# Second block's experts: eight in fixed places, twenty-four ranked on the chip and loaded by register, six pairs and five quads in place of sixteen pairs

## The chip, the core and the metric

The kernel runs on one core of one Trainium2 chip. The metric is the time of one execution on the device in microseconds; the change is compared with the kernel before it on the same chip.

A core has several engines, each with an instruction queue of its own that it works through in order: TensorE (PE; its weight loads are shown apart as PEld), VectorE (DVE), ScalarE (ACT), GpSimd (POOL) and SyncE (SP). SP issues nearly all transfers here. They run on the core's 16 DMA engines.

## What is computed

Two transformer blocks stand one behind the other, for 256 tokens of 1024 channels. The first has one layer, with 16 experts that choose their tokens. The second has two layers, and each ends in the mixture of experts that the change is about: every token picks one of four groups and two of that group's eight experts, each of which is a gated product with 256 hidden columns.

```python
def hier_moe(x, rg_w, rg_b, re_w, re_b, w_gate, w_up, w_down):
    ...
    lg = jnp.einsum('td,dg->tg', t, rg_w, ...) + rg_b
    g_star = jnp.argmax(lg, -1)
    ...
    top_v, top_i = lax.top_k(le, TOP_K_IN_GROUP)          # 2 of the group's 8
    ...
    for g in range(N_GROUPS):
        h = silu(einsum('td,edf->tef', t, w_gate[g])) * einsum('td,edf->tef', t, w_up[g])
        y = y + jnp.einsum('tef,efd->td', h * gate[:, g, :, None], w_down[g])
```

All values are float32. So 512 pairs of token and expert fall on 32 experts, 16 on average, and how many an expert gets is known only when the router has run. Every expert's weights are 3 MiB: 1 MiB each of gate, up and down, 96 MiB per layer.

## The kernel before

Each layer of the second block is a mixer (`mixer2`), the router (`route2_logits`, `route2`, L2031) and a round of experts (`moe2_round`, L2115). The round does not compute all tokens with all experts. It gives every expert `CAP` = 48 places, followed by 16 of no use, so that an expert takes 64 columns. If an expert has more tokens than 48, a further round runs over all experts (the loop at L2342); `nrounds` says how many, and all engines read it into a register at L2340 and branch at L2341.

Within a round:

- `gather(oc)`, for eight experts at a time: VectorE writes the one-hot matrix S (L2127) by comparing slot numbers with `key`, TensorE multiplies the tokens' two float32r parts xh and xl with it (tile `ga`), ScalarE and VectorE evacuate the result in turn to `xsT` (L2136, L2139).
- `onehot(qd)`, for four experts: S transposed (`GT`, copied to `G`) and the gates of the slots (`gs`).
- `gate_up(pr)`, for a pair of experts: 16 products that accumulate in one bank `pg`, the first expert's slots on partitions 0 to 63, the second's on 64 to 127. ScalarE and VectorE make `hid` of it (L2177, L2178). TensorE takes gate_up of the next pair ahead of the rest of this one.
- `hid_transposed(pr)`: two transposes (`hT`), copied by VectorE to `hidT` (L2186).
- `down(pr)`: 8 products into two banks `py`, evacuated in two float32r parts `yhl` (L2201, L2202) that are scaled with the gates.
- `scatter(pr)`: 8 products `sct` of G and yhl, which VectorE adds to `y` (L2216).

A float32 product of 512 columns shows as two records of 128x512 in the trace.

The weights come in loads of 1 MiB ([128, 2048] floats): per expert two for gate and up (half the rows each, gate and up side by side) and one for down. `loads2` (L2102) lists them in the order of use: gate and up of pair 0, then of each further pair with down of the pair before. `plan` takes the list; `fetch` issues some ahead into slots; `next_w` hands out the next load that was issued, or, once those are used up, issues one into the slot whose turn it is (`fetch_one`, L253). There are 17 slots in turn (nine `ring`, seven `ringb` and the tile XT2), and two tiles that serve once (`wx`). By the time the round starts, 19 loads have been issued. All further ones stand on SP's queue, each with a wait for the products that read its slot last.

Around the first gather, the order of work on all engines but SP is the scheduler's from the point `order.__exit__` on; what stands ahead of it stands in the order of the code. `residual` (L2317) makes `y` ALPHA times the layer norm's result in two halves, whose vectors are loaded; the second half's are issued from GpSimd. `gates` (L2076) works out the gates and `nrounds`; it is called by the first `onehot`.

The first block's experts (`moe1`) work in groups of four, each with 32 slots: four products side by side on 32 columns each. Their weights are loaded in the same slots.

## Time and profile before

| | us |
|---|---|
| three runs | 1740.32, 1737.74, 1728.4 |
| median | 1737.74 |
| span of the profiled execution | 1736.4 |

| engine | busy us | share of the span |
|---|---|---|
| PE | 1587.0 | 91% |
| PEld | 828.7 | 48% |
| DVE | 746.9 | 43% |
| ACT | 391.6 | 23% |
| POOL | 228.1 | 13% |

No time of the profiled execution other than its span is given. HBM was read at 286 GB/s over the span, 495 MB in all.

How to read the profile: the timeline lists instructions of an engine in order of time, like ones merged, with what ended an idle time in square brackets. A line number is that of the kernel; L308 is the helper through which all products go, L312 the one for transposes, so tiles tell them apart. Windows give each engine's busy time in a stretch, TensorE's granted clock (1.00 is the upper of its two levels), and the share and rate of the DMA engines. Products on TensorE are pipelined, so a busy TensorE is not one at its peak, and products side by side overlap in the records.

### The profile page before, as it was taken

The numbers are of one execution on the slowest core, as the hardware profiler recorded it, in microseconds if no ns is written. First come the engines' busy times: TensorE is split into PE (matmuls) and PEld (weight loads), VectorE is DVE, ScalarE is ACT, GpSimd is POOL, SyncE is SP. The second block draws the span as 40 slices with busy tenths as digits, with TensorE's granted clock in tenths as the row PEclk, the third lists the DMA queues.
The fourth block names the chain that finished last, engine by engine and source line by source line (L and its number), as shares of the span: only waits on it lengthen the run. The fifth ranks groups of instructions, "written<-read, shape, count | busy, mean of one in ns | idle before, by whom it ended". The sixth has DMA issues, their size and how long they took to land. (4 is left out here: it accounts for less than half of the span.)

```text
span 1736.4 us, 19979 instructions
## 1 busy us (share of the span) xinstructions
PE 1587.0 (91%) x7819; PEld 828.7 (48%) x7825; DVE 746.9 (43%) x1552; ACT 391.6 (23%) x740; POOL 228.1 (13%) x147
## 2 busy tenths in 40 slices
PE   8969899988898888899998999999899999999996
PEld 3738775221241221267777454343567875444432
DVE  6798774010010000189446343232796545433325
ACT  2443333000000000055443111111445432111101
POOL 2362531000000000031212000000231211000000
PEclk8879999999989999999999999999989999999998
DMA  8446666999999999933456899984243737998860
GB/s 350 170 131 245 259 262 260 417 418 418 417 417 418 417 419 418 393 116 146 169 207 242 327 377 360 374 338 156 77 149 122 278 124 305 376 408 340 343 271 25
DMA packets 110229, 497.49 MB, mean 287 GB/s; under 512 B 9082, under 2 KB 9719, under 8 KB 88874
## 3 DMA queue, kind: packets, MB, share of 16 engines
q1 hardware_dynamic: 108904, 492.75, 72.0%
q10 hardware_dynamic: 690, 2.10, 0.3%
q0 software_dynamic: 528, 1.23, 0.3%
q8 instruction: 65, 1.06, 0.2%
q14 instruction: 42, 0.34, 0.1%
HBM read 495.00 MB, written 1.05 MB: 286 GB/s over the span
## 5 line engine op out<-in xcount | busy, mean ns | idle before, releaser
L308 PE MATMUL pg<-w,xsT 128*64 128x512 f32 (+1 forms) x1504 | 375.2, 602 | 17.4 <-DMA w<-in_w_gate_dram 15.6
L308 PEld LDWEIGHTS pg<-w,xsT 128*64 128x64 f32 (+1 forms) x1504 | 105.2, 128 | 232.2 <-issue 184.7
L266 POOL TENSOR_TENSOR wl<-w,wh 128x1024 fp32r<-128x1024 f32 x47 | 116.9, 2487 | 363.4 <-ACT wh L265 250.6
L308 PE MATMUL py<-w,hidT 128*64 128x512 f32 x496 | 152.8, 601 | 3.7 <-DVE hid L2178 3.7
L308 PE MATMUL py<-w,hh 128*32 128x512 f32 x512 | 128.7, 599 | 25.0 <-DMA w<-in_w_down_dram 25.0
L308 PE MATMUL pu<-w,xsT 128*32 128x512 f32 x512 | 126.2, 598 | 19.8 <-DMA w<-in_w_up_dram 19.8
L265 ACT ACTIVATE wh<-w 128x1024 fp32r<-128x1024 f32 x98 | 103.1, 1059 | 128.9 <-PE pj L308 56.2
L308 PE MATMUL pj<-wh,xTp 128*128 128x512 f32 (+1 forms) x448 | 123.7, 407 | 0.9 <-ACT cn L1718 0.9
L1397 DVE TENSOR_TENSOR hh<-hh,pu 128x512 f32<-128x512 f32 x8 | 5.4, 686 | 218.4 <-PE pu L308 218.4
L266 DVE TENSOR_TENSOR wl<-w,wh 128x1024 fp32r<-128x1024 f32 x51 | 73.4, 1439 | 58.7 <-ACT wh L265 38.5
L2202 DVE SCALAR_TENSOR_TENSOR yhl<-py,gs,yhl 128x512 fp32r<-128x512 f32 x64 | 47.8, 749 | 107.5 <-ACT yhl L2201 107.5
L308 PEld LDWEIGHTS pj<-wh,xTp 128*128 128x128 f32 x448 | 80.8, 198 | 19.4 <-issue 3.6
L308 PEld LDWEIGHTS py<-w,hh 128*32 128x32 f32 x512 | 29.3, 108 | 120.5 <-DMA w<-in_w_down_dram 66.1
L2216 DVE TENSOR_TENSOR y<-y,sct 128x512 f32<-128x512 f32 x128 | 81.9, 681 | 10.6 <-PE sct L308 10.5
L1396 ACT ACTIVATE hh<-pg 128x512 f32<-128x512 f32 x8 | 4.8, 597 | 344.8 <-PE pg L308 234.1
L308 PEld LDWEIGHTS py<-w,hidT 128*64 128x64 f32 x496 | 47.2, 136 | 71.9 <-issue 53.7
L308 PE MATMUL sct<-yhl,G 128*128 128x512 f32 x256 | 78.6, 428 | 0.0
L2177 ACT ACTIVATE hid<-pg 128x256 f32<-128x256 f32 x32 | 12.3, 385 | 286.8 <-PE pg L308 286.8
L2201 ACT ACTIVATE yhl<-py,gs 128x512 fp32r<-128x512 f32 x64 | 43.8, 688 | 144.9 <-PE py L308 128.0
L308 PEld LDWEIGHTS pu<-w,xsT 128*32 128x32 f32 x512 | 28.3, 109 | 100.3 <-DMA w<-in_w_up_dram 51.3
L1421 DVE SCALAR_TENSOR_TENSOR y<-py,gs,m 128x512 f32<-128x512 f32 x8 | 6.0, 750 | 148.9 <-PE py L308 148.5
L308 PEld LDWEIGHTS sct<-yhl,G 128*128 128x128 f32 x256 | 41.6, 188 | 50.9 <-DVE y L2216 19.5
(638 smaller groups left out, 2426.3 us busy)
## 6 DMA issues: line engine op xcount, KB each, us to landing
w<-in_expert_w_gate_up_dram SPq DMA_DIRECT2D x126, 1024.0 KB, 8.5
w<-in_w_up_dram SPq DMA_DIRECT2D x64, 1024.0 KB, 18.0
w<-in_w_down_dram SPq DMA_DIRECT2D x64, 1024.0 KB, 18.1
w<-in_w_gate_dram SPq DMA_DIRECT2D x62, 1024.0 KB, 18.4
w<-in_expert_w_down_dram SPq DMA_DIRECT2D x62, 1024.0 KB, 7.0
w<-in_w_in_dram SPq DMA_DIRECT2D x38, 1024.0 KB, 4.9
wmod<-in_w_ada_dram SPq DMA_DIRECT2D x12, 1024.0 KB, 5.4
wmod<-in_w_ada_dram SPq DMA_DIRECT2D x13, 512.0 KB, 9.3
```

What stands on the lines that cost most here:

```text
L265: nc.scalar.activation(hi, src, AF.Copy)
L266: (eng or nc.vector).tensor_tensor(lo, src, hi.bitcast(F32), ALU.subtract)
L308: self.nc.tensor.matmul(out, lhsT, rhs, start=start, stop=stop)
L1396: nc.scalar.activation(hs, pg[nb], AF.Silu)
L1397: nc.vector.tensor_mul(hs, hs, pu[nb])
L1421: nc.vector.scalar_tensor_tensor(y[:, cs], py[nb], Gs[g][1], m5[:, cs], op0=ALU.mult, op1=ALU.mult)
L2177: nc.scalar.activation(hid, pg[:, 0:256], AF.Silu)
L2201: nc.scalar.activation(yh[:, c], py, AF.Copy, scale=gs[:, pr % 2:pr % 2 + 1])
L2202: nc.vector.scalar_tensor_tensor(yl[:, c], py, gs[:, pr % 2:pr % 2 + 1], yh[:, c].bitcast(F32), op0=ALU.mult, op1=ALU.subtract)
L2216: nc.vector.tensor_add(acc[:, t, c], acc[:, t, c], pt)
```

## The change

The 32 experts get places in an order of their own. Places 0 to 7 are experts 0 to 7, as before. Places 8 to 31 are the other 24 in the order of how many tokens they have, fullest first. Places 0 to 11 (the eight fixed and the four fullest) have 64 slots each and work in six pairs; places 12 to 31 have 32 slots and work in five quads, four experts side by side on 32 columns. Eleven groups take the place of sixteen.

The ranks are worked out by VectorE in `order` (in `route2`): a score of each expert, its comparison with the 23 others, the sum as rank, the 24 x 24 permutation, and by products with it and sums (`pick`) the experts' numbers `ids` in order and the columns of `key` (`keyd`). `gates` also makes the gates' columns in order (`gated`) and compares the counts with the rooms of 64 or 32 for `nrounds`.

The loads of places 8 to 31 need `ids`. `loads2` gives a function for each load; at the first load of a group of four places SP reads four numbers into registers (`TENSOR_LOAD ids`), and each load's address is worked out from one (an `ISA` row ahead of each). The down weights are laid out in DRAM as one run of 8 KB per partition instead of two of 4 KB. Gathers serve three groups (384 columns, as before), four per round; the one-hots are made for a group at a time, and the first scatter stands behind the second down. A further round, should one be needed, goes over all experts in 16 pairs of 64 slots.

```diff
-CAP = 48
+NS, NB, BIG, SMALL = 8, 4, 64, 32
+GROUPS = [(BIG, (i, i + 1)) for i in range(0, NS + NB, 2)] + [(SMALL, tuple(range(i, i + 4))) for i in range(NS + NB, 32, 4)]
+FURTHER = [(BIG, (i, i + 1)) for i in range(0, 32, 2)]
...
     def fetch_one(self):
         src, shape = self.todo.popleft()
+        if callable(src):
+            src = src()
...
+        def pick(out, src):
+            for i in range(0, n, n // 2):
+                js = slice(i, i + n // 2)
+                tm = q.tile([128, n // 2, n], F32, name="picked")
+                nc.vector.tensor_tensor(tm, perm[:, js], src[:, None, :].to_broadcast([128, n // 2, n]), ALU.mult)
+                nc.vector.tensor_reduce(out[:, js], tm, axis=AX.X, op=ALU.add)
+
+        def order():
+            sc = q.tile([128, 32], F32, name="score")
+            nc.vector.scalar_tensor_tensor(sc, count, 32.0, self.iota[:, 0:32], op0=ALU.mult, op1=ALU.subtract)
+            for i in range(0, n, n // 2):
+                js = slice(i, i + n // 2)
+                tm = q.tile([128, n // 2, n], F32, name="picked")
+                nc.vector.tensor_tensor(tm, sc[:, None, NS:].to_broadcast([128, n // 2, n]),
+                                        sc[:, NS:][:, js, None].to_broadcast([128, n // 2, n]), ALU.is_gt)
+                nc.vector.tensor_reduce(rank[:, js], tm, axis=AX.X, op=ALU.add)
+            nc.vector.tensor_tensor(perm, self.iota[:, 0:n, None].to_broadcast([128, n, n]),
+                                    rank[:, None, :].to_broadcast([128, n, n]), ALU.is_equal)
...
+            pick(idf, self.iota[:, NS:32])
+            nc.vector.tensor_copy(ids, idf)
+            for t in range(2):
+                pick(keyd[:, t], key[:, t, NS:])
...
         def gates():
...
             nc.vector.tensor_add(gate, oh[:, :, 0], oh[:, :, 1])
+            for t in range(2):
+                pick(gated[:, t], gate[:, t, NS:])
...
-    def loads2(self, l):
+    def loads2(self, l, groups, ids=None):
+        def expert(i):
+            if i < NS or ids is None:
+                return i
+            if i not in named:
+                c = i - NS
+                _, vs = nc.values_load_multi_w_load_instructions(
+                    ids()[0:1, c:c + 4], [mybir.EngineType.SP], min_val=NS, max_val=31, ...
+                named.update({i + j: v for j, v in enumerate(vs)})
+            return named[i]
...
+            return gu_[l, bass.ds(e, 1), h].rearrange("o p (k c) -> p (o k) c", k=4)
...
-        return gu(0) + [a for pr in range(1, 16) for a in gu(pr) + d(pr - 1)] + d(15)
+        return gu(0) + [a for g in range(1, n) for a in gu(g) + d(g - 1)] + d(n - 1)
...
-                wt = [self.next_w() for _ in range(2)]
+                wt = [self.next_w() for _ in places]
                 for k in range(4 * h, 4 * h + 4):
-                    for j in range(2):
-                        self.mm(pg[64 * j:64 * j + 64, :], xsT[:, k, (e + j) * CAP:(e + j) * CAP + 64], wt[j][:, k % 4, :],
-                                start=(k == 0), stop=(k == 7))
+                    for j, w in enumerate(wt):
+                        c = slice(n * j, n * j + n)
+                        self.mm(pg[c, :], xsT[:, k, c], w[:, k % 4, :], start=(k == 0), stop=(k == 7))
...
         gate_up(0)
+        if residual:
+            r.order()
+            r.gates()
         onehot(0)
...
-        for pr in range(16):
-            if pr < 15:
-                gate_up(pr + 1)
-            hidT = hid_transposed(pr)
-            if pr:
-                scatter(pr - 1)
-            if pr % 4 == 2 and pr < 14:
-                gather(pr // 4 + 1)
-            if pr % 2 == 0 and pr < 14:
-                onehot(pr // 2 + 1)
-            down(pr, hidT)
-        scatter(15)
+        for g in range(last + 1):
+            if g < last:
+                gate_up(g + 1)
+            hidT = hid_transposed(g)
+            if g > 1:
+                scatter(g - 1)
+            if g < last:
+                onehot(g + 1)
+            if g % 3 == 1 and g + 2 <= last:
+                gather(g + 2)
+            down(g, hidT)
+            if g == 1:
+                scatter(0)
+        scatter(last)
```

How this moves instructions is shown at three places of the first layer's round, the kernel before first and the changed kernel second each time. The first is VectorE's queue at the round's start, from the residual's second half to the copy `hidT` of the first group, for which the first down product waits. Before:

```order
L2328 SCALAR_TENSOR_TENSOR y_3855<-y_3855,gb_5821 128x512 x2
L2329 SCALAR_TENSOR_TENSOR y_3855<-gb_5821,y_3855 128x512
L2155 CAST G_5871<-GT_5872 128x512
L2161 COPY gs_5870<-gs_5878 128x2
L2329 SCALAR_TENSOR_TENSOR y_3855<-gb_5821,y_3855 128x512
L2178 TENSOR_TENSOR hid_5842<-hid_5842,pg_5825 128x256
L2186 COPY hidT_5915<-hT_5912 128x256
```

And in the change, from the first `hid` on:

```order
L2271 TENSOR_TENSOR hid_5847<-hid_5847,pg_5830 128x256
L2095 TENSOR_TENSOR picked<-perm,routes 128x288
L2254 COPY gs_5920<-gs_5926 128x1
L2427 SCALAR_TENSOR_TENSOR y_3855<-gb_5826,y_3855 128x512
L2096 TENSOR_REDUCE byrank_5743<-picked 128x12
L2426 SCALAR_TENSOR_TENSOR y_3855<-y_3855,gb_5826 128x512
L2095 TENSOR_TENSOR picked<-perm,routes 128x288
L2427 SCALAR_TENSOR_TENSOR y_3855<-gb_5826,y_3855 128x512
L2096 TENSOR_REDUCE byrank_5743<-picked 128x12
```

Behind these nine rows stand two more pairs of `picked` and `byrank_5743`, the second group's `hid`, and only then `hidT` of the first; ahead of them, from the first gather's last evacuation on, stand the rest of the ranking and the residual.

The second place is TensorE's queue from the first group's transposes on. Before:

```order
L312 MATMUL hT_5912<-ident,hid_5842 128x128 x2
L312 MATMUL GT_5919<-ident,S_5763 128x128 x4
L308 MATMUL gs_5925<-routes,S_5763 64x1 x8
L308 MATMUL py_5936<-w,hidT_5915 64x512 x4
L308 MATMUL py_5943<-w,hidT_5915 64x512 x4
L308 MATMUL pg_5950<-w,xsT_5764 64x512 x16
L312 MATMUL hT_5970<-ident,hid_5909 128x128 x2
L308 MATMUL pg_6006<-w,xsT_5764 64x512
```

In the change:

```order
L318 MATMUL hT_5956<-ident,hid_5847 128x128 x2
L318 MATMUL GT_5963<-ident,S_5769 128x128 x2
L314 MATMUL gs_5967<-routes,S_5769 64x1 x4
L314 MATMUL pg_5988<-w,xsT_5770 64x512
L314 MATMUL py_5974<-w,hidT_5959 64x512 x4
L314 MATMUL py_5981<-w,hidT_5959 64x512 x4
L314 MATMUL pg_5988<-w,xsT_5770 64x512 x15
L318 MATMUL hT_6008<-ident,hid_5953 128x128 x2
L318 MATMUL GT_6015<-ident,S_5769 128x128 x2
L314 MATMUL gs_6019<-routes,S_5769 64x1 x4
L314 MATMUL ga_6031<-S_6025,xh 128x384
```

The second gather (`ga_6031`) has moved ahead of the fourth group's gate-and-up and the second down, and stands right behind the one-hot products that read the S before it.

The third place is SP's queue from load 20 on. Before:

```order
L253 DMA w<-in_expert_w_gate_up_dram 128x2048
L253 DMA w<-in_expert_w_down_dram 128x2x1024 x2
L253 DMA w<-in_expert_w_gate_up_dram 128x2048 x4
L253 DMA w<-in_expert_w_down_dram 128x2x1024 x2
L253 DMA w<-in_expert_w_gate_up_dram 128x2048 x4
```

In the change:

```order
L259 DMA w<-in_expert_w_gate_up_dram 128x2048
L259 DMA w<-in_expert_w_down_dram 128x2048 x2
L2167 TENSOR_LOAD ids
L259 ISA
L259 DMA w<-in_expert_w_gate_up_dram 128x2048
```

Load 23 is the first behind a register load, and each load of a ranked expert has a register operation ahead of it. There are six `TENSOR_LOAD ids` per layer.

## Rows read from the trace of the kernel before

**Rows 1.** Cores: span and mean granted clock.
```profile
core 0: 1736.4 us, clock 0.967
```

**Rows 2.** Timeline of TensorE, first layer's round: start, duration, instruction, count, idle before.
```profile
952.54 0.43 PE L308 MATMUL ga<-S,xl 128*128 128x384 f32 x1
...
957.91 0.34 PE L308 MATMUL ga<-S,xl 128*128 128x384 f32 x1
958.18 7.09 PE L308 MATMUL pg<-w,xsT 128*64 128x512 f32 x32
...
973.28 0.44 PE L312 MATMUL hT<-ident,hid 128*128 128x128 f32 x2
...
974.58 3.65 PE L308 MATMUL py<-w,hidT 128*64 128x512 f32 x16
...
1020.98 2.10 PE L308 MATMUL sct<-yhl,G 128*128 128x512 f32 x8
```

**Rows 3.** Timeline of TensorE and VectorE where both rounds end and the second begins.
```profile
1218.79 3.65 PE L308 MATMUL py<-w,hidT 128*64 128x512 f32 x14
...
1223.88 2.56 DVE L2216 TENSOR_TENSOR y<-y,sct 128x512 f32<-128x512 f32 x4
...
1452.60 7.09 PE L308 MATMUL pg<-w,xsT 128*64 128x512 f32 x32
...
1718.31 2.56 DVE L2216 TENSOR_TENSOR y<-y,sct 128x512 f32<-128x512 f32 x4
```

**Rows 4.** Windows: length, engines' busy us (and count), clock, DMA share, GB/s.
```profile
600.00:640.00 40.00, 34.16 (x137) 8.72 (x136) 4.25 (x6) 0.00 (x0) 0.00 (x0) 1.00 1.02 418
...
980.00:1000.00 20.00, 19.16 (x80) 6.65 (x78) 5.06 (x9) 1.92 (x4) 0.21 (x1) 1.00 1.01 422
...
1040.00:1060.00 20.00, 19.94 (x77) 7.24 (x74) 7.77 (x14) 3.14 (x5) 0.00 (x0) 1.00 1.02 422
1060.00:1080.00 20.00, 19.70 (x100) 10.62 (x98) 4.93 (x10) 3.43 (x6) 0.20 (x1) 1.00 0.82 322
...
1460.00:1480.00 20.00, 19.90 (x123) 8.12 (x121) 6.26 (x14) 2.24 (x4) 0.00 (x0) 1.00 1.01 390
```

**Rows 5.** Waits of SP's queue, 958 to 1200: total us, times, longest.
```profile
SPq L253 <- PE pg L308: 129.7, 42, 21.6
```

**Rows 6.** Timeline of SP: the twentieth load of the first layer's round.
```profile
961.85 0.33 SPq L253 DMA_DIRECT2D w<-in_expert_w_gate_up_dram  x1
```

**Rows 7.** Timeline of TensorE in the first block: a quad's product waits for its tiles.
```profile
689.34 1.90 PE L308 MATMUL pu<-w,xsT 128*32 128x512 f32 x4 [0.62 <-DMA w<-in_w_up_dram]
691.80 3.62 PE L308 MATMUL pu<-w,xsT 128*32 128x512 f32 x20 [0.56 <-DMA w<-in_w_up_dram]
```

**Rows 8.** Timeline of TensorE: the ends of the sixth and the seventh gate-and-up.
```profile
1031.71 3.65 PE L308 MATMUL pg<-w,xsT 128*64 128x512 f32 x14
...
1051.46 0.59 PE L308 MATMUL pg<-w,xsT 128*64 128x512 f32 x1
```

**Rows 9.** Timeline of VectorE at the start of the first layer's round.
```profile
958.28 0.68 DVE L2136 TENSOR_SCALAR xsT<-ga,v2T 128x384 f32<-128x384 f32 x1 [0.73 <-PE ga L308]
...
960.92 0.69 DVE L2329 SCALAR_TENSOR_TENSOR y<-gb,y 128x512 f32<-128x512 f32 x1
968.13 1.29 DVE L2328 SCALAR_TENSOR_TENSOR y<-y,gb 128x512 f32<-128x512 f32 x2 [6.51 <-DMA gb<-in_ln_g_dram]
...
972.55 0.41 DVE L2178 TENSOR_TENSOR hid<-hid,pg 128x256 f32<-128x256 f32 x1
973.76 0.42 DVE L2186 COPY hidT<-hT 128x256 f32<-128x256 f32 x1 [0.79 <-PE hT L312]
...
975.10 1.28 DVE L2127 TENSOR_TENSOR S<-iota,routes 128x512 fp32r<-128x512 f32 x2
```

**Rows 10.** Line L2340, the register loads of nrounds: count, duration ns min/median/max.
```profile
L2340 SPq TENSOR_LOAD <-nrounds x2: 293/394/494, 1195.6 to 1673.7; - x2
L2340 SPq FUSED_REGOPS  x2: 164/172/181, 1196.1 to 1674.0; - x2
```

**Rows 11.** DMA issues: count, KB each, median us from issue to landing.
```profile
w<-in_w_in_dram SPq DMA_DIRECT2D x38, 1024.0 KB, 4.9
```

More of the change, by code (lines that the diff above doesn't have):

```diff
@@ L1555, in mixer2 @@
         late, nw = [], [0]
-        self.plan(self.loads2(l), 8)
+        self.plan(self.loads2(l, GROUPS, lambda: self.routes.ids), 8)
         def proj(c0, c1):
@@ L2115, in moe2_round @@
[L2115 to L2128 removed]
+        class Routes:
+            pass
@@ new lines, in moe2_round, with gather @@
+    def moe2_round(self, l, q, groups, r, xh, xl, acc, g_col, b_col, residual=None, extra=None, order=None):
+        nc, A = self.nc, self.A
+        further = groups is FURTHER
+        keys = (lambda t, i, m: r.all_keys[:, t, i:i + m]) if further else r.keys
+        gate = (lambda t, i: r.all_gates[:, t, i:i + 1]) if further else r.gate
+        xsTs, Ss, Gs = {}, {}, {}
+        last = len(groups) - 1
+        def gather(g0, then=None):
+            gs = range(g0, min(g0 + 3, last + 1))
+            m = 128 * len(gs)
+            S = self.cp.tile([128, 2, 384], F32R, name="S2", tag="gb")
+            xsT = q.tile([128, 8, 384], F32, name="xsT2", tag="xsT2")
+            for t in range(2):
+                g = g0
+                while g in gs:
+                    n, places = groups[g]
+                    e = g
+                    while e in gs and groups[e][0] == n and (further or (groups[e][1][0] < NS) == (places[0] < NS)):
+                        e += 1
+                    k = (e - g) * 128 // n
+                    Sv = S[:, t, (g - g0) * 128:(e - g0) * 128].rearrange("p (e c) -> p e c", c=n)
+                    nc.vector.tensor_tensor(Sv, self.iota[:, None, 32:32 + n].to_broadcast([128, k, n]),
+                                            keys(t, places[0], k)[:, :, None].to_broadcast([128, k, n]), ALU.is_equal)
+                    g = e
+            for g in gs:
+                c = slice((g - g0) * 128, (g - g0 + 1) * 128)
+                Ss[g], xsTs[g] = S[:, :, c], xsT[:, :, c]
@@ L2187, in hid_transposed, with down @@
             return hidT
-        def down(pr, hidT):
-            gs = Gs[pr // 2][1]
-            wd = [self.next_w() for _ in range(2)]
+        def down(g, hidT):
+            n, places = groups[g]
+            gs = Gs[g][1]
+            wd = [self.next_w() for _ in places]
             yhl = q.tile([128, 2, D], F32R, name="yhl2", tag="yhl2", bufs=2)
```

157 lines of the change are left out of this document (87 added, 70 removed).

## The prediction

> **What bounds the kernel now.** I began with the span of the core [rows 1] and then looked where the change lies: the second block runs its experts twice, once per layer, and each time over 268 us. The first stage begins with the first gate-and-up product at 958.18 and ends with the last addition at 1223.88 + 2.56 = 1226.44 us; the second runs from 1452.60 to 1718.31 + 2.56 = 1720.87 [rows 2, 3]. Both last 268.3 us, so 1736.4 - 2 x 268.3 = 1199.8 us lie outside, which the change leaves alone.
>
> The windows of the first stage come next [rows 4]. TensorE is busy in practically every microsecond at a granted clock of 1.00, while the DMA engines are full in some windows (422 GB/s) and not in others (322 GB/s). The loads wait for TensorE, not the other way round: SP, which issues the loads, spends 129.7 us of the stage waiting for gate-and-up products to leave a slot [rows 5]. So TensorE bounds the stage, and the loads are close behind.
>
> How close: a layer has 96 loads of 1 MiB. At 422 GB/s one takes 1.0486 / 0.422 = 2.485 us, so 96 take 239 us of a stage of 268. Nineteen have been issued before the stage; the twentieth goes at 961.85, when the first slot is free [rows 6].
>
> **What the change removes.** Sixteen groups per layer become eleven. From the stretch of rows [rows 2], one pair costs TensorE 7.0 us for gate and up (32 records at 7.09), 3.6 for down, 2.1 for scatter and 0.4 for the transposes, 13.1 in all. A quad runs four 32-column products side by side where a pair runs two of 64, so the same 7 us serve four experts, if the overlap is whole. The first block has quads already: there the last of four tiles lands and 20 records take 3.62 us [rows 7], which scaled to 64 records is at most 11.6 us, and at the pair's rate of work at least 7. Five groups fewer are some 65 us of TensorE less per layer. Either end leaves a quad far below its loads: twelve loads are 29.8 us, its TensorE work between 14 and 21. The removed 65 us therefore are not what is gained: DMA becomes the bound.
>
> **The floor that the loads set.** 77 loads from 961.85 on take 77 x 2.485 = 191.3 us and end at 1153.2. I allow 1 us from landing to the waiting product. From the last down product to the last addition the old stage takes 1226.44 - 1218.79 = 7.65 us [rows 3]; the new end looks the same. The floor is 1161.8, that is 64.6 us per layer saved and a total of 1736.4 - 129.2 + 1.3 = 1608.5 us. The 1.3 us are what the median of the runs lies above the span.
>
> **What holds the loads back.** I number them in the order of use. The ring takes 17 slots in turn and two tiles serve once, so load 52 takes the slot of load 35, which is the first of the first quad. While TensorE works through the six pairs it frees slots hardly faster than DMA fills them. When does it reach the first quad? Before, the sixth gate-and-up ends at 1031.71 + 3.65 = 1035.36 and the seventh at 1051.46 + 0.59 = 1052.05 [rows 8]; half of the seventh is done some 3.5 us earlier, at 1048.55. In the change two things come on top.
>
> First, one more gather lies in this stretch: gathers now serve three groups, so the second and the third stand ahead of the first quad where before one stood. A gather takes TensorE from 952.54 to 957.91 + 0.34, 5.7 us [rows 2].
>
> Second, VectorE gets the ranking. It is 24 operations of 288 elements, one of 576 and about a dozen small ones. The nearest row, 256 elements, takes 0.41 us [rows 9], so I take 0.42 for 288: 10.1 + 0.8 + 1.5, or 12.4 us. What of it lies on the path? As the order of instructions shows, 19 of the operations of 288 elements (8.0 us), 12 small ones (1.8), the eight of the residual (5.5), the first one-hot copy and both products of hid stand between the last evacuation of the first gather and the copy hidT, for which the first down product waits. The evacuation ends at 958.28 + 0.68 [rows 9], half a microsecond later after the change. The residual's second half waits for a transfer: before, it starts 6.5 us after the first half's end at 961.61. In the change the first half ends at about 963.1, the second starts at 969.6, and what stands from there on (2.1 us up to the first hid, 0.4 for it, 5.6 of residual and ranking, 0.4 for the second hid) brings hidT to about 978.1. Before, it started at 973.76 and down followed at 974.58 [rows 2, 9]. The first down is late by 4.3 us, and behind it on TensorE's queue stand all further products. Nothing else waits for VectorE in that time.
>
> Two smaller waits follow. The second gather now stands right behind the third group's one-hot products, and its S is computed only after these: four operations, by the row of two S [rows 9] about 1.3 us, with 0.4 to start. Before, S was computed under a down and two gate-and-ups. The first scatter, moved behind the second down, waits up to 1 us for its two parts. Together 7.0 us; at the low end none of it shows, at the high end the ranking costs twice as much and it is 14.
>
> So the first half of the first quad is consumed at 1048.55 + 5.7 + 7.0 = 1061.3. Load 52 lands at 1063.7; the 44 behind it run unhindered, since each slot was freed some 40 us before its turn, and end at 1063.7 + 44 x 2.485 = 1173.1. With 1 + 7.65 the stage ends at 1181.7: 44.7 us saved per layer. With none of the stalls it is 51.7, with twice of them 37.7. The second stage is the first moved by 494.4 us, row for row at both ends, and I count it the same. **Sum: 1736.4 - 2 x 44.7 + 1.3 = 1648.3 us**; its own range is 1634 to 1663.
>
> **Edits that I cost at nothing.** SP gets six register loads per layer and a register operation ahead of 74 loads. The trace has both at the end of a stage: 0.29 to 0.49 us and 0.17 us [rows 10]. With the issue of 0.33 us this stays under the 2.485 us that a load takes, which covers it. The first register load needs the ids. My sum has them on VectorE at 963.8 and SP comes there with load 23 at about 965.3, with loads 20 to 22 still under way until 969; an id 5 us late would still be covered. The down weights now lie in runs of 8 KB in place of two of 4 KB; full windows show 418 GB/s with the first block's 4 KB runs and 422 here [rows 4], so nothing follows. The memsets that go from GpSimd waited for others. The next layer's first loads used to be issued long before the end; now they queue behind load 96 and land some 6 us after it, ahead of the 7.65 us tail. ScalarE and VectorE lose evacuations with the five groups, under a bound that isn't theirs.
>
> **Rivals.** *The floor.* If the head's stalls fall into time in which DMA still has slots, the total goes toward 1608. For it speaks that in the windows between 980 and 1060 DMA was often full; against it that SP waits 129.7 us.
>
> *A lower rate or clock.* One window in which DMA is full gives only 390 GB/s [rows 4]: 2.69 us a load. 44 loads then take 9 us more per layer, 1666. TensorE at 1.2 GHz in the quads would double 14 us to 29, still under 29.8, and double the tail, so 1664. Against the clock: the first block's quads wait for loads in the same rhythm at a granted clock of 1.00 [rows 4, 7]. The Trainium skill (DMA: Bandwidth & Descriptors, Specifications) puts the memory's share of one core at about 358 GB/s, as an estimate 2.93 us a load and 1687 us; the 418 and 422 of the rows speak against it.
>
> *Slower than before: loads by register don't overlap.* No row here shows a weight loaded through a register. If each waited for the one ahead to land, it would cost what loads that come alone cost, a median of 4.9 us to landing [rows 11]. 74 x 4.9 from 966 on ends the stage at 1337, 111 us later than before, so 1960 us. It decides against the change from a spacing of 3.2 us on (2.485 + 44.7 / 60, over the quads' 60 loads). Against it: SP's issues take 0.33 us and have a queue of their own.
>
> *The change doesn't do what it says: a further round.* It runs where an expert has more tokens than its place holds: 64 for the eight fixed and the four fullest of the others, 32 for the rest. It would add some 268 us per layer. Routed through the reference, its own inputs give the fixed experts at most 16 and 23 tokens and the fifth fullest of the others 21 and 22, so it is not needed. Before, with 48 places, the fullest had 30 and 39.
>
> **How the numbers follow.** The forecast, quads bound by DMA after a head that holds it back (1634 to 1663), gets 0.57; toward the floor, down to 1608, 0.14; a lower rate, a lower clock or a longer head, 1663 to 1717, 0.19; next to no gain 0.04; register loads that don't overlap 0.05; a further round 0.01. The range 1614 to 1692 leaves out about a quarter of the second, a third of the third and the last three. Measurements of this kernel tell a change of about 1%, 17 us, from none: faster 0.9, within it 0.04, slower 0.06.
>
> **What would show it.** Right: in the windows from about 1065 to 1170 DMA is full at 418 to 425 GB/s, quads' products wait for transfers, gate-and-up products follow each other at about 30 us, and the stage ends near 1182, the second near 1631. The copy hidT of the first pair starts near 978. Wrong: register operations of over 2 us on SP, gaps of DMA within the quads, TensorE's clock at half there, or a stage that ends after 1200. If the head takes no longer than before, the second down starts before 992 and the floor is the better sum.

## The result, and the profile after

| | runs | median us | lowest to highest | ratio to the kernel before |
|---|---|---|---|---|
| before | 4 | 1736.11 | 1728.40 to 1740.32 | |
| changed | 4 | 1658.11 | 1649.42 to 1666.91 | 0.9544, interval 0.9512 to 0.9577 |
| changed, measured again in a later set | 6 | 1650.06 | 1648.41 to 1655.38 | 0.9517, interval 0.9491 to 0.9544 |

The change makes the kernel faster by 4.6 to 4.8%. The forecast was 1648.3 us with a range of 1614 to 1692. The profiled execution of the changed kernel has a span of 1647.7 us.

The bounds of both stages, as in [rows 2, 3]: TensorE's first gate-and-up product and VectorE's last addition.

```profile
950.62 7.09 PE L314 MATMUL pg<-w,xsT 128*64 128x512 f32 x32
...
1176.03 2.55 DVE L2309 TENSOR_TENSOR y<-y,sct 128x512 f32<-128x512 f32 x4
...
1404.47 7.09 PE L314 MATMUL pg<-w,xsT 128*64 128x512 f32 x32
...
1629.42 2.55 DVE L2309 TENSOR_TENSOR y<-y,sct 128x512 f32<-128x512 f32 x4
```

The first stage lasts 1176.03 + 2.55 - 950.62 = 228.0 us, the second 227.5, where both took 268.3. So 40.3 and 40.8 us are saved; the forecast said 44.7 for each.

Both taken from 1736.4 would leave a span of 1655.3. That of this execution is 7.6 us shorter, since the first stage begins at 950.62 and not at 958.18 [rows 2], behind code that the change doesn't edit. Products of the first block that are the same in both kernels already stand 10 us earlier, and in the first microseconds TensorE had more of its clock. Of the kernel before, a group of instructions by line (count, duration in ns, first and last start) and two windows (columns as in [rows 4]); then the same of the changed kernel:

```profile
L308 PE MATMUL pos<-sel,tri x6: 262/263/283, 285.8 to 286.4; 128*128 128x16 f32 x6
```

```profile
20.00:40.00 20.00, 16.64 (x46) 5.43 (x44) 15.41 (x19) 6.53 (x12) 7.34 (x3) 0.78 1.03 416
40.00:60.00 20.00, 18.84 (x90) 9.79 (x90) 12.55 (x44) 5.51 (x11) 2.27 (x2) 0.67 0.23 83
```

```profile
L314 PE MATMUL pos<-sel,tri x6: 262/263/283, 275.8 to 276.4; 128*128 128x16 f32 x6
```

```profile
20.00:40.00 20.00, 15.69 (x71) 5.73 (x69) 17.86 (x39) 7.25 (x13) 6.08 (x3) 1.00 1.03 417
40.00:60.00 20.00, 16.73 (x113) 11.72 (x112) 14.88 (x33) 10.68 (x18) 7.67 (x6) 0.91 0.22 83
```

This is a matter of the execution and not of the change: the run e6 below, whose code up to the round is that of the changed kernel, had 0.77 and 0.67 of the clock in these windows and the same products at 289.1. So a single execution can gain or lose 10 us before the experts begin. The lengths of the two stages carry little of this (in a second execution of the changed kernel 229.2 and 226.8 us), and below they are read beside the times.

The windows that answer to [rows 4], in the first stage:

```profile
980.00:1000.00 20.00, 18.69 (x94) 10.35 (x92) 9.11 (x19) 5.61 (x9) 0.00 (x0) 1.00 1.01 426
...
1040.00:1060.00 20.00, 20.00 (x134) 9.18 (x131) 7.59 (x14) 4.15 (x7) 0.00 (x0) 1.00 0.77 288
1060.00:1080.00 20.00, 19.80 (x133) 6.83 (x136) 5.64 (x11) 2.14 (x4) 0.00 (x0) 1.00 1.01 425
...
1100.00:1120.00 20.00, 14.97 (x101) 5.04 (x100) 5.39 (x11) 2.23 (x4) 0.00 (x0) 1.00 1.01 426
```

From 1060 on DMA is full at 425 to 426 GB/s, and soon TensorE has idle time: the bound has changed sides, as forecast. Between 1040 and 1060 DMA has a gap, 288 GB/s, while TensorE has none. Ahead of it, DMA is full too, and that was not expected. SP's queue tells why. Its timeline before; then, of the changed kernel, the first of its waits from 820 to 951 us (total, times, longest) and its timeline:

```profile
879.17 0.61 SPq L2323 DMA_DIRECT2D gb<-in_ln_g_dram  x1
879.82 0.44 SPq L2323 DMA_DIRECT2D gb<-in_ln_b_dram  x1
883.93 0.81 SPq L253 DMA_DIRECT2D w<-in_expert_w_gate_up_dram  x2
```

```profile
SPq L2421 <- PE rt L314: 62.2, 1, 62.2
```

```profile
933.16 0.33 SPq L2421 DMA_DIRECT2D gb<-in_ln_g_dram  x1
933.54 1.17 SPq L2421 DMA_DIRECT2D gb<-in_ln_b_dram  x1
934.76 0.90 SPq L259 DMA_DIRECT2D w<-in_expert_w_gate_up_dram  x2
```

The residual's first vectors now wait 62.2 us for products of the router, and 13 of the 19 loads that run ahead stand behind them on SP's queue. (The expectations below call them loads 5 to 19; they are 7 to 19.) The first of them starts at 934.76 in place of 883.93, the last at 951.86 in place of 939.79, and they keep DMA busy into the stage. The change edits neither the vectors nor their place on the queue. It puts new tiles into the pool that holds theirs, so that theirs may lie where the router's products still read; this is argued from the code and was not tried apart. One of the new tiles, `picked`, is not needed for it: e2 below has none, and the wait is 62.2 us there too.

### The profile page after: what moved, and what is told of

Same layout as the page of the kernel before. It is cut to its first block, busy times and chain, and to the rows that moved or that the text cites. A ratio compares the mean times of both kernels' runs of the same rounds, so it can differ in the third digit from the quotient of the medians.

```text
span 1647.7 us, 19894 instructions
## 1 busy us (share of the span) xinstructions
PE 1460.6 (89%) x7699; PEld 766.0 (46%) x7705; DVE 713.9 (43%) x1550; ACT 373.1 (23%) x710; POOL 226.1 (14%) x139
## 5 line engine op out<-in xcount | busy, mean ns | idle before, releaser
L314 PE MATMUL pg<-w,xsT 128*32 128x512 f32 (+1 forms) x1504 | 316.1, 621 | 36.4 <-DMA w<-in_expert_w_gate_up_dram 20.8
L314 PEld LDWEIGHTS pg<-w,xsT 128*32 128x32 f32 (+1 forms) x1504 | 80.0, 120 | 227.6 <-issue 139.0
L314 PE MATMUL py<-w,hidT 128*32 128x512 f32 (+1 forms) x496 | 122.2, 614 | 15.1 <-DVE hidT L2279 6.0
L271 ACT ACTIVATE wh<-w 128x1024 fp32r<-128x1024 f32 x98 | 103.2, 1060 | 128.8 <-PE pj L314 52.7
L2296 DVE SCALAR_TENSOR_TENSOR yhl<-py,gs,yhl 128x512 fp32r<-128x512 f32 x44 | 32.6, 749 | 91.8 <-ACT yhl L2295 91.8
L314 PEld LDWEIGHTS py<-w,hidT 128*32 128x32 f32 (+1 forms) x496 | 32.1, 122 | 84.5 <-issue 48.3
L2270 ACT ACTIVATE hid<-pg 128x256 f32<-128x256 f32 x22 | 8.5, 385 | 252.5 <-PE pg L314 252.4
L314 PE MATMUL pj<-wl,xTp 128*128 128x512 f32 (+1 forms) x224 | 60.6, 393 | 0.3 <-DVE wl L272 0.3
L2309 DVE TENSOR_TENSOR y<-y,sct 128x512 f32<-128x512 f32 x88 | 56.1, 681 | 3.6 <-PE sct L314 3.0
L314 PE MATMUL ga<-S,xh 128*128 128x384 f32 (+1 forms) x160 | 51.0, 337 | 5.4 <-DVE S L2220 5.4
L2295 ACT ACTIVATE yhl<-py,gs 128x512 fp32r<-128x512 f32 x44 | 29.8, 687 | 113.3 <-PE py L314 109.8
```

The source lines that it names most:

```text
L271: nc.scalar.activation(hi, src, AF.Copy)
L314: self.nc.tensor.matmul(out, lhsT, rhs, start=start, stop=stop)
L2270: nc.scalar.activation(hid, pg[:, 0:256], AF.Silu)
L2295: nc.scalar.activation(yh[:, c], py, AF.Copy, scale=gs)
L2296: nc.vector.scalar_tensor_tensor(yl[:, c], py, gs, yh[:, c].bitcast(F32), op0=ALU.mult, op1=ALU.subtract)
L2309: nc.vector.tensor_add(acc[:, t, c], acc[:, t, c], pt)
```

## The experiments

All edits are to the changed kernel. The stage lengths are from the one profiled execution of each; the ratio is to the kernel before in the same set of runs.

| run | first, second stage us | median us | ratio, interval |
|---|---|---|---|
| changed | 228.0, 227.5 | 1658.1 | 0.9544 (0.9512 to 0.9577) |
| changed again (e5) | 229.2, 226.8 | 1650.1 | 0.9517 (0.9491 to 0.9544) |
| e1 fixed addresses | 223.9, 223.3 | 1646.2 | 0.9478 (0.9453 to 0.9503) |
| e2 no ranking | 222.9, 220.9 | 1643.1 | 0.9459 (0.9423 to 0.9496) |
| e3 early loads | 225.6, 224.9 | 1651.9 | 0.9505 (0.9478 to 0.9533) |
| e4 interleaved | 222.6, 222.1 | 1646.9 | 0.9493 (0.9465 to 0.9522) |
| e6 code order | 223.8, 224.4 | 1653.1 | 0.9507 (0.9471 to 0.9544) |
| e7 interleaved, early | 221.7, 222.6 | 1644.0 | 0.9480 (0.9453 to 0.9507) |
| e8 all | 220.1, 219.8 | 1641.6 | 0.9460 (0.9433 to 0.9486) |
| e9 short head | 214.9, 214.6 | 1629.0 | 0.9380 (0.9358 to 0.9402) |
| e10 three pairs first | 219.6, 217.2 | 1634.9 | 0.9423 (0.9401 to 0.9444) |
| e11 short head, fixed | 213.0, 213.6 | 1630.0 | 0.9381 (0.9358 to 0.9403) |
| e12 short head, pairs first | 217.0, 216.6 | 1634.7 | 0.9414 (0.9389 to 0.9439) |

### Do loads by register cost anything?

```diff
         def expert(i):
-            if i < NS or ids is None:
-                return i
+            return i
```

> The changed kernel, with every load's address written in as a constant: places 8 to 31 load the experts 8 to 31 in order, no register is read and no register operation stands ahead of a load; the ranking is still worked out. So the weights of the ranked places are those of other experts than their tokens chose. Theory (the forecast's): register loads are covered by the 2.46 us that a load takes, so the time stays within 0.5% of the changed kernel's 1658 us (1650 to 1666), about 0.954 of the kernel before. Rival: addresses from registers cost something on the path, at 0.2 us or more for each of 44 loads behind the first quad: 9 us per layer or more, 1640 us or less.

The stages came out 4.1 us shorter, which neither theory had. TensorE suggests another reason than registers: the scheduler had laid the products in another order. Timeline of TensorE between the fourth and the sixth pair, the changed kernel and then e1:

```profile
1010.50 4.46 PE L314 MATMUL pg<-w,xsT 128*64 128x512 f32 x18
...
1015.72 3.65 PE L314 MATMUL pg<-w,xsT 128*64 128x512 f32 x14
...
1021.37 1.91 PE L314 MATMUL py<-w,hidT 128*64 128x512 f32 x4
...
1023.47 3.65 PE L314 MATMUL py<-w,hidT 128*64 128x512 f32 x12
```

```profile
1014.93 7.04 PE L314 MATMUL pg<-w,xsT 128*64 128x512 f32 x32
...
1024.61 3.64 PE L314 MATMUL py<-w,hidT 128*64 128x512 f32 x16
```

The same 32 records take 4.46 + 3.65 = 8.1 us when a transpose and two records of scatter cut them, and 7.0 in one piece; the 16 of down take 5.6 and 3.6. In the run e5 the changed kernel had the same cuts again, with 18 and 14 and with 4 and 12 records, so the order belongs to the program and not to the run. It is less the cut that costs than the running side by side that is lost: the piece of four records takes 1.91 us, 0.48 each, because its records start one after another, while the 16 in one piece run in pairs and take 0.23 each. The two cuts make 3.0 us; the first quad began 98.9 us after the stage's start in e1, 102.3 in the changed kernel.

> The changed kernel itself, a second time, beside the others of this set. The run with fixed addresses had stages of 223.9 and 223.3 us, the first run of the changed kernel 228.0 and 227.5. Theory (TensorE's order, which the scheduler makes anew for each program, sets the time to the first quad): the same program gives the same stages, 227 to 229 us, and a time within 0.4% of 1658 us. Rival (the difference is one of runs, not of programs): stages of about 224 us and a time of about 1647 us.

The stages, 229.2 and 226.8 us, are within 1.2 us of the first run's and belong to the program, as the theory said. The time, 1650 us, was nearer to the rival's: the medians of two sets of the same kernel differ by the 8 us in question.

The question was asked again where TensorE's order is fixed: e11 makes the same edit to e9, the fastest version (below).

> The run with the short head and interleaved groups (215 us per stage, 1629 us), with every load's address written in as a constant, as in the first run of this study; so the ranked places load other experts than their tokens chose, the rest is the same. TensorE stands in the order of the code in both, so the scheduler cannot move its products this time. Theory: register loads cost nothing on the path, the stages stay at 214 to 216 us and the time within 0.3% of 1629 us. Rival: the 4 us per stage that constants were worth in the first run come from the registers and show again: 210 to 212 us per stage, 1621 us.

The times are the same, 1630.0 and 1629.0 us. The stages are 1.9 and 1.0 us shorter with constants, a little below the theory's range, where two executions of the changed kernel differ by 1.2 and 0.7; so 1 to 2 us per stage may hang on registers and the order of the other engines, or on nothing, but not the 4 of the rival. The rows say the same: a register load takes 0.30 us, and of the operations ahead of each transfer the longer takes 0.05 us (lines of SP, changed kernel; durations in ns):

```profile
L2167 SPq TENSOR_LOAD <-ids x12: 295/300/514, 959.9 to 1565.3; - x12
L259 SPq FUSED_REGOPS  x144: 37/46/61, 960.5 to 1602.3; - x144
```

### Does the ranking lie on the path?

```diff
-                pick(keyd[:, t], key[:, t, NS:])
+                nc.vector.tensor_copy(keyd[:, t], key[:, t, NS:])
...
-                pick(gated[:, t], gate[:, t, NS:])
+                nc.vector.tensor_copy(gated[:, t], gate[:, t, NS:])
```

> As the kernel with fixed addresses, and the ranking is left out too: two copies of 24 columns stand for the 16 products and sums, the permutation is a memset, and the room of every place counts as 64; so VectorE has some 11 us less to do at each round's start, and tokens beyond 32 of an expert in a quad are lost. Theory: TensorE's first down product no longer waits 3.1 us for hidT, and what is behind it comes earlier by as much, up to the load that waits for the first quad's slots and with it to the stage's end: 3 to 5 us per layer, 1648 to 1652 us. Rival (the head's stalls fall into time that DMA spends on loads that are late anyway, since loads 5 to 19 are issued only from 934.76 us on): less than 1 us per layer, within 0.2% of the run with fixed addresses.

TensorE's wait for hidT, 2.92 us in e1, went, and the first quad began 94.4 us after the stage's start instead of 98.9 in e1. The stages followed by only 0.9 and 2.4 us: DMA, which e1 left with a gap, was full in every 10 us of this stage, so the loads that start late had become the bound. The rival was nearer.

### The late loads, and the order of the groups

```diff
-                            (nc.gpsimd if nb else nc.sync).dma_start(r[:, i], ...
+                            nc.gpsimd.dma_start(r[:, i], ...
```

> The changed kernel, with the residual's first two vectors issued by GpSimd's queue instead of SP's, where their wait of 62.2 us held back the loads 5 to 19. Theory of the slots (the forecast's): TensorE waits for no load before the first quad, so its pace and the slot of load 52 stay, and the time stays within 0.4% of the changed kernel's 1658 us; the idle time of DMA only moves, from ahead of the stage into it, between 960 and 1055. Rival: the late loads are what holds the stage, since DMA is full from 940 to 1040; loads that start 40 us earlier then shorten each stage by more than 6 us, 1645 us or less.

The last of the 19 loads was issued at 940.03 us instead of 951.86, and the time, 1651.9 us, is that of the changed kernel (1650.1 and 1658.1). The theory of the slots holds: TensorE sets when slots come free, and the late loads only hid it; with the loads early, DMA falls to 143 GB/s between 1000 and 1010. The stages are 2 to 3 us shorter; since the scheduler changed TensorE's order here as well, that part is not assigned.

```diff
+ORDER = (0, 1, 2, 3, 6, 4, 7, 5, 8, 9, 10)
+GROUPS = [GROUPS[g] for g in ORDER]
```

> The changed kernel with its eleven groups in another order: the four fixed pairs, then quad, pair, quad, pair and three quads, in place of six pairs and five quads. The sums are the same. Theory of the slots: the gap of DMA between 1040 and 1060 (288 GB/s over 20 us in place of 425, that is 6.4 us of it lost) comes from pairs that free slots slower than loads fill them; with a quad after four pairs the gap closes, DMA is full from 940 to the stage's end, and each stage is 5 to 7 us shorter: 1644 to 1648 us. Rival: the gap has another cause or comes back elsewhere, and the time stays within 0.3% of 1658 us.

The gap closed, as the theory said (windows of e4):

```profile
1040.00:1060.00 20.00, 18.49 (x83) 8.72 (x84) 5.93 (x16) 2.74 (x5) 0.00 (x0) 1.00 1.01 425
```

The stages fell by 5.4 us, to 222.6 and 222.1; what is left is DMA without a gap from 960 on, about the stage's start (959.48).

Both edits together, e7:

> Both edits at once: the groups as four pairs, quad, pair, quad, pair, three quads, and the residual's vectors on GpSimd's queue, so that loads 5 to 19 start some 40 us earlier. Alone they took 5.4 and 2.5 us from a stage of 227.7. Theory: with the groups interleaved DMA has no gap left from 940 us on, so the late start of the loads is now what bounds the stage, and starting them earlier is worth more than it was alone: 212 to 219 us per stage, 1628 to 1640 us. Rival: gains add at most, 219 to 222 us and 1642 to 1647 us, since slots are freed no sooner by TensorE.

The rival was right: 221.7 and 222.6 us. With the loads early the gaps came back elsewhere, at 179 GB/s in the stage's first 10 us and 214 to 315 between 40 and 70 us, because TensorE freed slots no sooner. So two bounds lie close together here: loads that start late, and slots that come free late. Taking away one shows the other.

### What holds TensorE at the head

```diff
-        for g in range(last + 1):
+        with self.tc.manual_schedule(engines={mybir.EngineType.PE}) if residual else nullcontext():
+            for g in range(last + 1):
...
-            if g % 3 == 1 and g + 2 <= last:
-                gather(g + 2)
-            down(g, hidT)
-            if g == 1:
-                scatter(0)
+                down(g, hidT)
+                if g == 1:
+                    scatter(0)
+                if g % 3 == 1 and g + 2 <= last:
+                    gather(g + 2)
```

> The changed kernel with TensorE's products of the round in the order of the code instead of the scheduler's, and each further gather behind the down product that it stood ahead of; registers and ranking as in the change. Theory: products that are cut into pieces by others cost time (32 records of one gate-and-up take 7.0 us in one piece, 8.1 in two; 16 of down 3.6 and 5.6), and the first quad begins 3 to 6 us earlier than 100.5 us after the stage's start; the end follows, 222 to 225 us per stage, 1648 to 1652 us. Rival: pieces fill waits that a fixed order leaves empty, so the first quad begins no earlier and the time stays at 1658 us or rises.

The stages answer the theory: 223.8 and 224.4 us. The first quad begins at 1055.51 - 963.80 = 91.7 us of the stage, in one piece and more than the theory's 3 to 6 us ahead of 100.5, and DMA has no gap around it (timeline of TensorE and a window, both of e6):

```profile
1055.51 7.07 PE L314 MATMUL pg<-w,xsT 128*32 128x512 f32 x64
```

```profile
1040.00:1080.00 40.00, 40.00 (x302) 19.49 (x302) 17.28 (x34) 6.59 (x11) 0.00 (x0) 1.00 1.01 425
```

The time, 1653.1 us, does not show the gain. The profiled execution (1656.4 us) entered the stage at 963.80, 13 us later than the changed kernel's, in code that both share and with the low clock named above. All six executions have a lower mean granted clock (0.948 to 0.956) than those of e5 in the same set (0.959 to 0.963); why is open.

e8 joins e7 and e6, and moves the picks for the gates behind the second group's transposes in the code (`rest` is the second half of `gates`):

```diff
+        def rest():
             for t in range(2):
                 pick(gated[:, t], gate[:, t, NS:])
...
                 hidT = hid_transposed(g)
+                if residual and g == 1:
+                    r.rest()
```

> As the run before, with TensorE's order that of the code too, each further gather behind the down product, and the gates' eight products and sums by rank behind the second group's transposes, so that hidT of the first waits for less. Theory: TensorE's time to the first quad and the waits of the head are now what holds the slots back; 4 to 7 us per stage less than the run before: 207 to 214 us, 1618 to 1632 us. Rival: DMA is already full from the first free slot, so nothing more comes of it.

220.1 and 219.8 us: less was gained than the theory wanted. The edit of the picks did not do what it was for. VectorE's order is the scheduler's, and all the picks still stood ahead of hidT, for which TensorE now waited 4.90 us. e9 therefore fixes VectorE's order at the head too, and computes S of a further gather ahead of the down product that it stands behind; `order` keeps rank, permutation and ids, and `rest` holds the picks of keys and gates, the rooms and `nrounds`:

```diff
+        with self.tc.manual_schedule(engines={mybir.EngineType.PE, mybir.EngineType.DVE}) if residual else nullcontext():
+            if residual:
+                r.order()
+                r.gates()
+            gate_up(0)
+            onehot(0)
+            gate_up(1)
+            hidT = hid_transposed(0)
+            onehot(1)
+            if residual:
+                r.rest()
+                next(residual)
```

> The run with all edits (groups interleaved, loads early, TensorE in the order of the code), and VectorE too in the order of the code at the round's start: rank, permutation and ids, then hid and hidT of the first groups, then the picks by rank of keys and gates and the residual's second half, which stood ahead of hidT; S of a further gather is computed ahead of the down product it stands behind. Theory: TensorE's 4.9 us of waiting for hidT go, and with them the low clock of the products behind it (16 records of the first down took 6.2 us in place of 3.6); the slots come free 7 to 8 us earlier, DMA's gaps between 40 and 70 us of the stage shrink, and the stage falls from 220 to 211 to 215 us, the time to 1624 to 1634 us. Rival: the transfer of the residual's vectors or the wait of yhl for its room takes the stall's place, and the stage stays at 218 to 221 us.

214.9 and 214.6 us, 1629.0 us: the theory's numbers. The first down product in the timelines of TensorE, of the changed kernel, of e8 and of e9; for e8 and e9 with windows behind it:

```profile
970.26 5.19 PE L314 MATMUL py<-w,hidT 128*64 128x512 f32 x16 [3.10 <-DVE hidT L2279]
```

```profile
976.03 6.21 PE L316 MATMUL py<-w,hidT 128*64 128x512 f32 x16 [4.90 <-DVE hidT L2282]
```

```profile
975.00:985.00 10.00, 8.97 (x30) 2.76 (x32) 1.37 (x5) 0.00 (x0) 0.00 (x0) 0.69 0.92 364
```

```profile
973.14 3.65 PE L316 MATMUL py<-w,hidT 128*64 128x512 f32 x16 [0.43 <-DVE hidT L2283]
```

```profile
997.00:1007.00 10.00, 10.00 (x52) 5.66 (x52) 2.30 (x4) 2.02 (x3) 0.00 (x0) 1.00 0.65 248
1007.00:1017.00 10.00, 10.00 (x68) 4.15 (x68) 5.04 (x10) 1.76 (x3) 0.00 (x0) 1.00 0.82 331
1017.00:1157.00 140.00, 116.96 (x783) 47.62 (x775) 41.21 (x85) 16.68 (x29) 0.00 (x0) 0.99 1.01 425
```

The wait is paid twice: 4.90 us of waiting, and 16 records that then take 6.21 us instead of 3.65, in a window where the granted clock was 0.69. With 0.43 us of waiting they take 3.65. Together that is 7.0 us of TensorE, and the stages fell by 5.2; e9 makes several edits at once, and their shares were not tried apart. e9 still has a gap of DMA between 997 and 1017, and one at its start (179 GB/s from 957 to 967).

```diff
-ORDER = (0, 1, 2, 3, 6, 4, 7, 5, 8, 9, 10)
+ORDER = (0, 1, 2, 6, 3, 7, 4, 8, 5, 9, 10)
...
-            self.fetch(c, extra[0], a, XT2, extra[1])
+            self.fetch(c, extra[0])
...
                 r.order()
+                self.fetch(a, XT2, extra[1])
```

> As the run before, with the first quad in the fourth place instead of the fifth: three fixed pairs, quad, pair, quad, pair, quad, pair, two quads. Loads 17 to 19 are then of ranked experts and are issued once the ids are known. Theory: a quad frees eight slots with the same 7 us of TensorE in which a pair frees four, so the slots come free a group sooner: 2 to 4 us per stage less than the run before, 208 to 213 us. Rival: three loads that wait for the ids start so late that the gain is lost: 211 to 216 us.

At 219.6 and 217.2 us neither range holds. What the rival named came, and cost more than it said: the loads that wait for the ids were issued from 967.80 us on, and DMA had almost nothing to do from 952 to 972 (SP's timeline, then windows, both of e10):

```profile
941.50 0.42 SPq L261 DMA_DIRECT2D wx<-in_expert_w_down_dram  x1
967.80 0.95 SPq L261 DMA_DIRECT2D w<-in_expert_w_gate_up_dram  x2
```

```profile
952.00:962.00 10.00, 10.00 (x45) 8.81 (x45) 5.95 (x14) 2.13 (x4) 0.00 (x0) 0.70 0.00 2
962.00:972.00 10.00, 10.00 (x56) 3.67 (x56) 7.15 (x24) 2.64 (x5) 1.08 (x2) 1.00 0.34 72
```

The last run gives e9 the order of the change again:

```diff
-GROUPS = [GROUPS[g] for g in ORDER]
```

> The run with the short head and early loads, with the groups in the order of the changed kernel: six pairs, then five quads. Theory of the slots (the forecast's mechanism): the first quad begins at 88 to 92 us of the stage in place of 57, load 52 waits for its first half, and DMA has gaps again ahead of it; 2 to 5 us per stage more than with interleaved groups, 217 to 220 us, 1633 to 1639 us. Rival: once the head is short the order of the groups is worth nothing, 214 to 216 us.

217.0 and 216.6 us, 1634.7 us: the order of the groups is worth some 2 us per stage where the head is short, at the theory's lower end. DMA falls to 378 GB/s between 1044 and 1054, around the first quad's gate-and-up, where the theory put a gap; that is 1.1 us of it. The larger gap ahead, 293 and 333 GB/s between 994 and 1014, is one that e9 has too. e9 is the fastest version: 1629.0 us against 1650 to 1658 of the changed kernel.

## Why the prediction was right

The forecast said: DMA becomes the bound, after a head that holds it back. The traces agree with the mechanism, and 1658.1 and 1650.1 us lie 0.6 and 0.1% above 1648.3. That the second comes so near is in part luck: all four stages are 3 to 6 us longer than the forecast's 223.5, and the early starts of these executions, 950.62 and 952.42, give 6 to 8 us back. By its steps:

**The quads.** A quad's gate-and-up takes 7.07 us (e6, 64 records), the lower end of 7 to 11.6. The last two gate-and-ups begin 1136.94 - 1107.89 = 29.1 us apart, forecast as about 30, and TensorE waits for loads in them. Those ahead follow at 16 to 24 us and wait for no load.

**The head.** Two rows of VectorE, and the window of TensorE's first down, of the changed kernel:

```profile
962.11 0.69 DVE L2426 SCALAR_TENSOR_TENSOR y<-y,gb 128x512 f32<-128x512 f32 x1 [4.12 <-DMA gb<-in_ln_g_dram]
...
969.78 0.42 DVE L2279 COPY hidT<-hT 128x256 f32<-128x256 f32 x1
```

```profile
970.00:972.00 2.00, 1.74 (x4) 0.53 (x6) 0.60 (x3) 0.00 (x0) 0.00 (x0) 0.50 1.01 422
```

The residual's second half was forecast to start 969.6 - 958.18 = 11.4 us after the stage's start, held by its vectors' transfer; it started after 962.11 - 950.62 = 11.5, held by it. hidT was forecast after 19.9 us (978.1 - 958.18) and came after 969.78 - 950.62 = 19.2. S held the second gather by 1.31 us where 1.7 stood; of the 1.0 for the first scatter nothing shows. Two things in this part were not in the sum: the low clock after the wait (5.19 - 3.65 = 1.5 us, with a granted clock of 0.50 at its start), and the cut products (1.1 and 1.9 us). Cuts stood in the order of instructions ahead of the run, where they could have been counted, but no row priced them. In sum, load 52 was issued at 1055.76, that is after 105.1 us, where 103.1 was forecast.

**The mis-sized term** is the next one: "half of the first quad is consumed at 1061.3. Load 52 lands at 1063.7". This gave the load 2.4 us from issue to landing, the spacing of a full queue. But the queue had a gap at this moment, and a load that comes into a gap takes longer. The issue of load 52 on SP's timeline, and the DMA issues of the changed kernel in windows around single loads (50, 51, 55, 56, 57 and 96; the last column is us from issue to landing):

```profile
1055.76 0.33 SPq L259 DMA_DIRECT2D w<-in_expert_w_gate_up_dram  x1
```

```profile
w<-in_expert_w_gate_up_dram SPq DMA_DIRECT2D x1, 1024.0 KB, 4.8
...
w<-in_expert_w_gate_up_dram SPq DMA_DIRECT2D x1, 1024.0 KB, 8.1
...
w<-in_expert_w_down_dram SPq DMA_DIRECT2D x1, 1024.0 KB, 10.2
...
w<-in_expert_w_down_dram SPq DMA_DIRECT2D x1, 1024.0 KB, 11.3
...
w<-in_expert_w_gate_up_dram SPq DMA_DIRECT2D x1, 1024.0 KB, 14.1
...
w<-in_expert_w_down_dram SPq DMA_DIRECT2D x1, 1024.0 KB, 20.4
```

Load 50 meets an empty queue and takes 4.8 us; load 51, issued 0.6 us behind it, takes 8.1. The issues list no landing for load 52 itself. Load 55, issued at 1057.70, lands at 1067.9; three steps of 2.48 back, load 52 lands at 1060.5, 4.7 us after its issue. [rows 11] had this price, 4.9 us for loads that come alone; it was used for a rival only. The Trainium skill (DMA: Bandwidth & Descriptors, Anatomy of one DMA) states a fixed part of about 2 us beside the moving of the bytes, as an estimate 4.4 us for 1 MiB; it gives this for another kind of queue, and the rows here show somewhat more, 4.7 to 4.9.

So the landing is 2.0 + 2.3 = 4.3 us later than forecast. Load 57, issued at 1060.12, lands at 1074.2, 3.7 us behind load 56 (1059.19 + 11.3), for a reason not looked for; load 96, issued at about 1150.6, lands at 1171.0, and the 39 steps from 57 to 96 are 2.48 us each. The 44 loads behind load 52 thus take 1171.0 - 1060.5 = 110.5 us, forecast 109.3, and from the last landing to the end it takes 1178.58 - 1171.0 = 7.6 in place of 8.65. 223.5 + 4.3 + 1.2 - 1.1 = 227.9: the stage as measured, 228.0.

Two slips change nothing in the sum. The prediction counts 74 loads with a register operation; the trace has 144 in both layers, 72 each, and only that rival's price hangs on it. It prices its dozen small VectorE operations at 1.5 us in one place and 1.8 in another.

**What was hidden.** "Nineteen have been issued before the stage" was read from the kernel before. In the changed kernel the last 13 of them were issued between 934.76 and 951.86, around the stage's start; the prediction looked at SP's queue only behind load 20. The late loads cost almost nothing in the changed kernel because TensorE's pace at the head left DMA time to catch up until 1040; the gap between 1040 and 1060, 20 x (1 - 288 / 425) = 6.4 us, is nearly all the time that DMA lost between 940 and the last landing. By this account the rival called the floor needs correcting too: with these late loads a stage could not have been much shorter than 228.0 - 6.4 = 221.6 us, and e2, e4 and e6, which leave the loads late, stop near it. The 203.6 us of the rival (1161.8 - 958.18) would want early loads and slots that are always free; the best version here stands at 214.7.

**The rivals.** A lower rate did not come: 425 GB/s, 2.48 us a load. The 358 GB/s of the Trainium skill (DMA: Bandwidth & Descriptors, Specifications) would have given 1687 us, by the prediction's estimate; every full window speaks against it for a core that runs alone. A lower clock in the quads showed in places (0.83 and 0.91 in windows between 1120 and 1160) and cost nothing there, since loads were the bound. Register loads overlap: e11. No further round ran. Between the stages nothing moved: 1404.47 - 1178.58 = 225.9 us, before 226.2.

**Left open.** Full windows show 425 to 426 GB/s where the kernel before had 418 and 422. Whether the 8 KB runs of the down weights do this was not tried; over 44 loads it is about 1 us. Open too are why the residual's first vectors wait for the router, and why e6's shorter stages do not show in its time.

## What to carry to other kernels

Where a change hands the bound from one engine to the transfers, look up when each slot is freed and when each transfer that runs ahead is issued, on the queue of the changed kernel from the first row on: one small transfer that waits can hold a queue, and 13 loads on it, for 62 us. Price a transfer that meets an empty queue by its whole landing time, and one in a full queue by its spacing. And when a small edit moves the time by a few microseconds, compare the order of the products before blaming the edit; fix that order by hand before pricing anything else.

## What the runs showed of the hardware

- A stall of TensorE is paid again in its clock, though not by its length: after 0.43 us of waiting the same 16 records took 3.65 us, after 3.10 and 4.90 us they took 5.19 and 6.21, at a granted clock of 0.50 at first. In e5, the changed kernel a second time, they took 6.46 behind nearly the same wait:

```profile
972.02 6.46 PE L314 MATMUL py<-w,hidT 128*64 128x512 f32 x16 [3.06 <-DVE hidT L2279]
```

- Products that run side by side on parts of the columns lost 1.1 to 1.9 us when others cut them so that some ran without a neighbour (7.0 to 8.1 and 3.6 to 5.6 us).
- A transfer whose address comes from a register costs SP 0.30 us for four addresses and some 0.05 us for the longer of two operations ahead of each transfer, and flows at 425 GB/s like any other.
- 1 MiB takes 4.7 to 4.9 us from issue to landing where it meets an empty queue, 8.1 where it comes 0.6 us behind another, and 2.48 us of spacing where the queue is full.
